# Turning an image batch by 180 degrees: the first store without its hold, all groups in four pieces

## The chip, the cores and the metric

The kernel runs on one core of one Trainium2 chip. The metric is the device time of one execution in microseconds (us). Before the change it is 121.88 us, the median of 3 runs (121.86 to 121.97). The tables and quoted lines below come from one profiled execution of the same kernel.

## What is computed

The input `x` is a float32 array of shape (32, 3, 256, 256), 25.17 MB. Each of the 96 images is turned by 180 degrees:

```python
def reference(x):
    return np.rot90(x, k=2, axes=(-2, -1)).astype(np.float32)
```

An image has 65536 numbers in a row in memory, and turning it by 180 degrees reverses that row from end to end. Nothing is added or multiplied: 25.17 MB are read, put in reverse order and written.

## The kernel before, in words

The 96 images are handled as three groups of 32. A group is held in one SBUF tile of 128 partitions by 16384 numbers (`A`, `Bt`, `Ct`, 64 KB in each partition, 8.39 MB in all): an image is cut into four quarters, and each quarter lies in a partition of its own. A fourth, small tile `T` is the scratch space.

**Loads.** All are issued at the very start (`load`, line 49). Group A comes in two DMAs: the first 512 numbers of every partition through ScalarE's queue (256 KB), the rest (7936 KB) through SyncE's queue. Groups B and C follow with one DMA each on SyncE's queue.

**Turning.** VectorE (DVE) reverses each partition in place. `turn` cuts the half row of 8192 numbers into pieces, and for each piece `swap` makes three copies (`copy`, line 44): the mirrored piece from the right end goes reversed into `T`, the piece from the left goes reversed to the right end, and `T` goes to the left. With four pieces a piece is 2048 numbers and a group takes 12 copies; with six pieces it is 1366 numbers (1362 for the last) and a group takes 18 copies. The copies keep the order in which the program names them: group A, then B, then C.

**Stores.** `store` (line 52) writes a whole group to the output with one DMA on SyncE's queue. Its address pattern runs through the four quarters of each image backwards, so that reversed quarters in reversed order make a reversed image. So every large transfer, the three loads and the three stores, is issued by SyncE and stands in its queue, `q1` in the profile; only the 256 KB piece of group A goes through ScalarE's queue, `q10`.

**What sets the order.** Semaphores that the framework puts in hold each copy until its group is loaded, and each store until its group is turned. One thing is written by hand: `add_manual_dep` makes the store of group A wait for the last copy of group B as well. This is the hold. In the program, the stores of A and B stand ahead of the turning of group C, and SyncE takes its stores in the order A, B, C, so a store that waits also keeps those behind it waiting.

Of the kernel before, what the change touches and what calls it, by code (L numbers as in the profile page):

```python
# [2 lines left out]

os.environ.setdefault("NEURON_RT_ULTRASERVER_MODE", "4")

# [4 lines left out]


@with_exitstack
def kernel(
    ctx: ExitStack,
    tc: tile.TileContext,
    x: bass.AP,
    out: bass.AP,
):
    nc = tc.nc  # L20
    P = 128

    B, C, H, W = x.shape
    L = H * W
    G = 32
    E = L // 4
    J = E // 8

    x4 = x.rearrange("b c h w -> (b c) (h w)").rearrange(
        "(g n) (s e) -> g (n s) e", n=G, s=4)  # L30
    o4 = out.rearrange("b c h w -> (b c) (h w)").rearrange(
        "(g n) (s e) -> g n s e", n=G, s=4)

    pool = ctx.enter_context(tc.tile_pool(name="slots", bufs=1))
    A = pool.tile([P, E], x.dtype, tag="A")
    Bt = pool.tile([P, E], x.dtype, tag="B")
    Ct = pool.tile([P, E], x.dtype, tag="C")
    T = pool.tile([P, J], x.dtype, tag="T")

    def back(t, lo, hi):  # L40
        return t[:, hi - 1:(lo - 1 if lo else None):-1]

    def copy(dst, src):
        c = nc.vector.tensor_copy(out=dst, in_=src)  # L44
        tc.keep_in_program_order(c)
        return c

    def load(t, g, lo=0, hi=E, queue=nc.sync):
        return queue.dma_start(out=t[:, lo:hi], in_=x4[g][:, lo:hi])  # L49

    def store(t, g):
        return nc.sync.dma_start(out=o4[g][:, ::-1, :], in_=t[:, :])

    def swap(t, lo, w):
        hi = E - lo - w
        copy(T[:, 0:w], back(t, hi, hi + w))
        copy(t[:, hi:hi + w], back(t, lo, lo + w))
        return copy(t[:, lo:lo + w], T[:, 0:w])

    half = E // 2  # L60

    load(A, 0, 512, E)
    load(A, 0, 0, 512, nc.scalar)
    load(Bt, 1)
    load(Ct, 2)

    def turn(t, pieces):
        step = -(-half // pieces)
        for lo in range(0, half, step):
            last = swap(t, lo, min(step, half - lo))  # L70
        return last

    turn(A, 4)
    last = turn(Bt, 6)
    tc.add_manual_dep(
        store(A, 0).ins, last.ins.name,
        mybir.DependencyInfo(
            mybir.DependencyClass.Sync, mybir.DependencyReason.DATA),
        reason="the first store goes when the loads are nearly done")
    store(Bt, 1)  # L80
    turn(Ct, 4)
    store(Ct, 2)


# [1 line left out]
_INS = ['x']  # L86
_OUTS = [((32, 3, 256, 256), 'float32')]


# [23 lines left out]
```

## Time and profile before

| what | value |
|---|---|
| median of 3 runs | 121.88 us |
| the three runs | 121.86, 121.88, 121.97 us |
| span of the profiled execution, first to last instruction | 120.1 us (120.07) |
| median less span | 1.8 us |
| VectorE busy | 45.2 us (38%), 42 copies |
| DMA queue q1 | 50.07 MB, 96.9% of the 16 DMA engines' span |
| DMA queue q10 | 0.26 MB, 0.6% |
| moved by DMA in all | 50.33 MB, 419 GB/s over the span |
| copies of group A | 22.69 to 37.79 us, 12 of 1.23 us |
| copies of group B | 42.11 to 58.40 us, 18 of 0.87 us |
| copies of group C | 61.45 to 76.56 us, 12 of 1.23 us |
| stores issued | A 58.43, B 59.10, C 76.59 us |

All times within an execution count from the start of its span. The profiled execution has no separate time of its own in the record beside its span; the medians are of other executions, and the 1.8 us between are what lies ahead of the first and behind the last instruction. A DMA's "us to landing" runs from the start of its issue until its semaphore is full, so it holds the time in which it stands behind other transfers. Besides the views, the trace holds a record of each DMA packet: its queue, size, start and duration. "Packet records" below means these, with the starts counted from the start of the span.

### The profile page before, as it was taken

To read this page: it belongs to the slowest core of one execution; us is meant where nothing else is said; L and a number is where in the kernel's file an instruction comes from. 1 tells how busy PE (TensorE), PEld (TensorE's weight loads), DVE (VectorE), ACT (ScalarE), POOL (GpSimd) and SP (SyncE) were. 2 spreads that over 40 slices of the span, in tenths; PEclk is the share of its full clock that TensorE was granted. 3 is DMA by queue.
4 is the path that set the end of the run, shared out by engine and by line. 5 is a ranking of instruction groups with operands and counts; after the bars stand their busy time and mean duration, and the time that the engine had idled before them with its cause. 6 is when DMAs were issued, how large, how long until landed. Compare 5 with 4: busy or idle time off the path is not lost.

```text
span 120.1 us, 99 instructions
## 1 busy us (share of the span) xinstructions
DVE 45.2 (38%) x42; POOL 0.2 (0%) x4
## 2 busy tenths in 40 slices
DVE  0000000499995099999459999400000000000000
POOL 0000000000000000000000000000000000000000
DMA  9888988899889988998899889988898889888980
GB/s 338 349 349 349 699 349 349 360 633 415 349 349 589 459 349 349 568 480 349 349 502 546 349 349 458 589 349 349 349 699 349 349 349 699 349 349 349 677 371 0
DMA packets 1008, 50.33 MB, mean 419 GB/s; under 512 B 112, under 2 KB 112, under 8 KB 240
## 3 DMA queue, kind: packets, MB, share of 16 engines
q1 hardware_dynamic: 864, 50.07, 96.9%
q10 hardware_dynamic: 144, 0.26, 0.6%
HBM read 25.17 MB, written 25.17 MB: 419 GB/s over the span
## 4 chain that ended last, share of the span: by engine, by line
DMA 34%; DVE 26%; another core or an unknown queue 2%; issue 1%; SPq 0%; DVEq 0%
DMA Bt<-in_x_dram 34%; DVE Bt L44 9%; DVE T L44 9%; DVE Ct L44 8%; SPq L49 0%; DVEq L44 0%
## 5 line engine op out<-in xcount | busy, mean ns | idle before, releaser
L44 DVE COPY T<-A 128x2048 f32<-128x2048 f32 x4 | 4.9, 1227 | 22.8 <-DMA A<-in_x_dram 22.7
L44 DVE COPY T<-Bt 128x1366 f32<-128x1366 f32 (+1 forms) x6 | 5.2, 873 | 4.5 <-DMA Bt<-in_x_dram 4.3
L44 DVE COPY T<-Ct 128x2048 f32<-128x2048 f32 x4 | 4.9, 1227 | 3.2 <-DMA Ct<-in_x_dram 3.1
L44 DVE COPY Bt<-T 128x1366 f32<-128x1366 f32 (+1 forms) x6 | 5.2, 873 | 0.2
L44 DVE COPY Bt<-Bt 128x1366 f32<-128x1366 f32 (+1 forms) x6 | 5.2, 872 | 0.2
L44 DVE COPY Ct<-T 128x2048 f32<-128x2048 f32 x4 | 4.9, 1227 | 0.1
L44 DVE COPY A<-T 128x2048 f32<-128x2048 f32 x4 | 4.9, 1227 | 0.1
L44 DVE COPY Ct<-Ct 128x2048 f32<-128x2048 f32 x4 | 4.9, 1227 | 0.1
L44 DVE COPY A<-A 128x2048 f32<-128x2048 f32 x4 | 4.9, 1226 | 0.1
L97 POOL MEMSET const-bfloat16-1.0<- 128x1 bf16 x1 | 0.1, 102 | 0.0
L97 POOL MEMSET const-uint8-127<- 128x1 uint8 x1 | 0.1, 102 | 0.0
L97 POOL MEMSET const-float32-0.0<- 128x1 f32 x1 | 0.1, 98 | 0.2 <-issue 0.2
L97 POOL MEMSET const-float32-1.0<- 128x1 f32 x1 | 0.1, 98 | 0.0
## 6 DMA issues: line engine op xcount, KB each, us to landing
A<-in_x_dram SPq DMA_DIRECT2D x1, 7936.0 KB, 21.9
A<-in_x_dram ACTq DMA_DIRECT2D x1, 256.0 KB, 22.1
Bt<-in_x_dram SPq DMA_DIRECT2D x1, 40.8
Ct<-in_x_dram SPq DMA_DIRECT2D x1, 59.7
out_dram<-A SPq DMA_DIRECT2D x1, 22.2
out_dram<-Bt SPq DMA_DIRECT2D x1, 40.9
out_dram<-Ct SPq DMA_DIRECT2D x1, 42.7
```

What stands on the lines that cost most here:

```text
L44: c = nc.vector.tensor_copy(out=dst, in_=src)
L97: nc = _bacc.Bacc("TRN2", target_bir_lowering=False, num_devices=1)
```

## The change

The hold is taken away, group B is turned in four pieces as the others are, and the three stores stand behind all copies in the program, in the order A, B, C. Each store then waits for its own group alone. No DMA is added, removed or resized, and each stays on its queue; VectorE makes 36 copies in place of 42.

```diff
     turn(A, 4)
-    last = turn(Bt, 6)
-    tc.add_manual_dep(
-        store(A, 0).ins, last.ins.name,
-        mybir.DependencyInfo(
-            mybir.DependencyClass.Sync, mybir.DependencyReason.DATA),
-        reason="the first store goes when the loads are nearly done")
+    turn(Bt, 4)
+    turn(Ct, 4)
+    store(A, 0)
     store(Bt, 1)
-    turn(Ct, 4)
     store(Ct, 2)
```

## The prediction

> **What bounds the kernel now.** I read the page first: the busy shares, the slices, the DMA queues.
>
> ```profile
> span 120.1 us, 99 instructions
> ...
> DVE  0000000499995099999459999400000000000000
> ...
> DMA  9888988899889988998899889988898889888980
> ...
> q1 hardware_dynamic: 864, 50.07, 96.9%
> ```
>
> The DMA row is full from the first slice to the last but one, while VectorE (DVE) has holes and stops at 76.56 us. So the 16 DMA engines are the bound. Next the DMA issues, with their time to landing, and the timeline around the hold:
>
> ```profile
> Bt<-in_x_dram SPq DMA_DIRECT2D x1, 40.8
> Ct<-in_x_dram SPq DMA_DIRECT2D x1, 59.7
> out_dram<-A SPq DMA_DIRECT2D x1, 22.2
> out_dram<-Bt SPq DMA_DIRECT2D x1, 40.9
> out_dram<-Ct SPq DMA_DIRECT2D x1, 42.7
> ```
>
> ```profile
> 1.18 0.43 SPq L49 DMA_DIRECT2D Bt<-in_x_dram  x1
> 1.65 0.43 SPq L49 DMA_DIRECT2D Ct<-in_x_dram  x1
> ...
> 36.56 1.23 DVE L44 COPY A<-T 128x2048 f32<-128x2048 f32 x1
> ...
> 57.53 0.87 DVE L44 COPY Bt<-T 128x1362 f32<-128x1362 f32 x1
> 58.43 0.63 SPq L52 DMA_DIRECT2D out_dram<-A  x1
> 59.10 0.59 SPq L52 DMA_DIRECT2D out_dram<-Bt  x1
> 61.45 1.23 DVE L44 COPY T<-Ct 128x2048 f32<-128x2048 f32 x1 [3.05 <-DMA Ct<-in_x_dram]
> ...
> 76.59 0.54 SPq L52 DMA_DIRECT2D out_dram<-Ct  x1
> ```
>
> Issue plus time to landing gives the landings: load B 42.0, load C 61.35, store A 80.6, store B 100.0, store C 119.3 us. Each is 19.3 to 19.4 us after the one ahead of it, although B and C were issued half a microsecond apart and store C at 76.59. So the DMAs of SyncE's queue run strictly one after the other, and each takes 19.3 us.
>
> The packet records say why. On each engine a DMA is eight packets of 64 KB and one of 4 bytes that raises the semaphore; a 64 KB packet follows the one before it after 2.414 us, in the loads and in the stores, and 8 x 2.414 = 19.31 us. From one DMA to the next an engine loses 6 to 10 ns. The first packet starts at 1.76 us, the last semaphore packet at 118.93 us, and nothing lies idle between. The chain of waits names the loads and VectorE but leaves out the stores; I take the queue's order instead.
>
> **The change, part by part.**
>
> *The hold goes.* Store A waits then for the copy that starts at 36.56 and lasts 1.23 us, so it is issued at about 37.82 us, 20.6 us earlier. Its first packet can start about 1.03 us after the issue (load A: issued at 0.73, first packet at 1.76), at 38.85 us. But at 38.85 the queue still holds the end of load B and all of load C, whose last semaphore packets start at 60.46 (first engine) to 60.87 us. If the queue keeps its order, store A's packets start where they start now. Now store A is issued at 58.43 and ready at 59.46, 1.0 us ahead of 60.46: the hold leaves no gap that could be closed. Saved: 0.
>
> *Group B in four pieces.* Now 18 copies take 58.40 - 42.11 = 16.29 us. Group A's 12 copies show the new price: 36.56 + 1.23 - 22.69 = 15.10 us. Group B would be turned at 42.11 + 15.10 = 57.21 us, 1.2 us earlier, and store B issued there rather than at 59.10. Its packets are needed when store A's are through, some 19.3 us after 60.46, at 79.8 us. Cover: 21 us. Saved on the path: 0. The copies themselves do not slow the packets: those of load B that ran beside group A's copies took 2.418 us each, the same as those of load B that ran while VectorE waited from 37.79 to 42.11 us.
>
> *The stores stand behind group C's copies in the program.* This matters only to the engine that runs both, and none does: copies are on VectorE, stores on SyncE. Nothing else waits behind the three stores there but the end of the kernel. VectorE starts group C when load C lands, 61.4 us, as now; group C is turned at 76.56 and its store is needed when store B's packets end, 79.8 + 19.3 = 99.1 us. Cover: 99.1 - 77.6 = 21.5 us.
>
> *How much stands in the queue.* At 1.65 us the queue held three loads, 24 large packets for each engine. After the change at most the end of load B, load C and store A stand there, some 18; later load C's end with stores A and B, fewer still. So no depth is reached that the trace has not shown.
>
> *A cost that the trace does not show:* a store waiting for 20 us behind loads. Nearest rows: when store A was issued, the load packets under way (start 58.02 to 58.46 us) took 2.439 to 2.444 us on four engines, not 2.418, and the first store packet took 2.455 us on one. If this is the price of a store that stands in the queue, it would be paid by the nine packets between 38.85 and 60.46: 9 x 0.026 = 0.23 us at the most, or 9 x 0.037 = 0.33 us by the other row. The other end is below nothing: those 22 to 37 ns are no longer paid at the join. I take 0, the row nearest to it being stores B and C, which stand behind other stores for 20 us and whose neighbours still come every 2.414 us.
>
> **Sum:** 0 + 0 + 0 against the span of 120.07 us; with the 1.8 us around it this is the median, 121.88 us. The forecast is no change.
>
> **The rivals.**
>
> *1. The store shares the engines with the loads (slower).* If store A does not queue behind load C but takes turns with it, load C lands late and group C is turned late. For this: packets of different queues do take turns. At the start the small ScalarE packets and the large SyncE packets alternate on every engine, and a ScalarE packet even slips in between the last data packet of load A and its semaphore packet. Against it: load and store have the same queue, q1. And at the join store A, ready at 59.46, would have found load C's last data packet ending at 60.46 and would have gone ahead of load C's semaphore packet; on all 16 engines the semaphore packet came first. Price: load B's data ends 2.4 us later (43.96), and load C then runs at half speed, 2 x 19.31 us, to 82.6 and lands at 83.0. Turned 15.15 us later (98.2), its store is ready at 99.2. The stores A and B keep the engines busy until 99.5, as the work is the same in any order. So with simple turns it costs nothing, with 0.3 us to spare; this is the point from which it decides. If store B is a third party from 60.7 us on, load C's data ends at 91.1, group C is turned at 106.7, its store ready at 107.7: a gap of 8.2 us, so 130.1 us.
>
> *2. A standing store stretches the load packets.* The price is above: up to 0.33 us, 122.2 us. For it are the four stretched packets; against it that the other 12 engines showed 4 ns at the most.
>
> *3. Store A starts reading while the load still writes (faster).* If an engine could read SBUF for the next store while it writes the last of a load, a store known earlier gains. Now store A is ready 1.0 us ahead of the join, so whatever lies within 1.0 us is already had; at most the rest of one packet, 2.4 - 1.0 = 1.4 us, is left: 120.5 us. Against it: an engine's packets at the join follow without overlap (semaphore packet at 60.457, store packet at 60.466 us), as at the joins between loads and between stores, where the successor stood ready for 20 us and more. The Trainium skill has a rule for this side: "DMA: Bandwidth & Descriptors", section "Two DMAs through the same engine are not ordered", says that descriptors of one queue start in order but are pipelined, with separate queues for reading and writing. By it the time could be 120.5 us; the trace agrees with the order of starts, and shows no overlap worth more than some 10 ns at any join, which would leave 121.88.
>
> *4. The change does not do what it says.* The stores now stand behind group C's copies. Should the framework let store A wait for the copies named last rather than for its own group's, it goes at 76.6: the engines idle from 60.9 to 77.6, and the time is 121.88 + 16.7 = 138.6 us. Against it: the first copy of group A starts at 22.69, on its own load, although loads B and C were named before it.
>
> **How the numbers follow.** Forecast, nothing moves: 0.46 (121.65 to 122.1). Rival 1: 0.22, of which 0.04 costs nothing and 0.18 lies evenly between 122.1 and 130.1. Rival 2: 0.14, of which 0.04 stays within the bound. Rival 3: 0.13, of which 0.03 within the bound. Rival 4: 0.05. About 0.2%, 0.24 us, is what a measurement of this kernel can tell from no change. Within it: 0.46 + 0.04 + 0.04 + 0.03 = 0.57; slower: 0.18 + 0.10 + 0.05 = 0.33; faster: 0.10. The range from 120.5 to 124.0 takes in the forecast, rivals 2 and 3, and the cheap part of rival 1 (0.04 and a quarter of 0.18): 0.46 + 0.14 + 0.13 + 0.04 + 0.04 = 0.81. The dear end of rival 1 and rival 4 are left out.
>
> **What would show it.** Right: store A issued at 37.8 with about 42.8 us to landing; store B at 57.2 with some 42.8 us; loads B and C landing at 42.0 and 61.35 as now; packets of 2.414 us throughout. Rival 1: load C lands well after 61.35, and VectorE's hole ahead of group C grows. Rival 2: load packets between 38.85 and 60.46 above 2.418 us. Rival 3: store A lands before 80.6. Rival 4: store A issued at 76.6. I am wrong if any transfer of the queue overtakes another.

## The result and the profile after

The changed kernel takes 122.84 us (median of 3 runs, 122.76 to 122.90) against 121.88 us: 0.96 us slower, a ratio of 1.0075 with a 95% interval from 1.0061 to 1.0088. The profiled execution took 122.76 us with a span of 121.03 us, 0.97 us more than before. The page after, in the lines that answer to those shown of before:

```profile
span 121.0 us, 94 instructions
...
DVE  0000000499994099998039999500000000000000
...
DMA  9888988897779877978989977997799779877980
...
q1 hardware_dynamic: 864, 50.07, 96.8%
```

```profile
Bt<-in_x_dram SPq DMA_DIRECT2D x1, 40.8
Ct<-in_x_dram SPq DMA_DIRECT2D x1, 60.6
out_dram<-A SPq DMA_DIRECT2D x1, 43.8
out_dram<-Bt SPq DMA_DIRECT2D x1, 43.7
out_dram<-Ct SPq DMA_DIRECT2D x1, 42.7
```

Its timeline around the stores:

```profile
37.78 0.63 SPq L52 DMA_DIRECT2D out_dram<-A  x1
...
57.21 0.55 SPq L52 DMA_DIRECT2D out_dram<-Bt  x1
62.34 1.23 DVE L44 COPY T<-Ct 128x2048 f32<-128x2048 f32 x1 [5.15 <-DMA Ct<-in_x_dram]
...
77.46 0.54 SPq L52 DMA_DIRECT2D out_dram<-Ct  x1
```

Stores A and B are issued when the prediction said, 37.78 and 57.21 us, and the queue keeps its order. Load B still needs 40.8 us to landing. But load C needs 60.6 us in place of 59.7, and everything behind it is late by as much: group C starts at 62.34 rather than 61.45 us, and store C is issued at 77.46 rather than 76.59. From load C's landing at 62.25 the stores land at 81.6, 100.9 and 120.2 us, 19.3 us apart as before. So the whole loss arises ahead of load C's landing and behind load B's.

The DMA view of 56 to 66 us shows where. It is cut into 40 slices of 0.25 us, and a packet's bytes are booked where it ends, so each burst is the end of one packet on all 16 engines. Before:

```profile
GB/s 524 0 0 0 0 0 0 0 2359 1835 0 0 0 0 0 0 0 786 2097 1311 0 0 0 0 0 0 0 1835 1573 786 0 0 0 0 0 0 0 2359 1835 0
```

After:

```profile
GB/s 524 0 0 0 0 0 0 0 1573 2621 0 0 0 0 0 0 0 0 0 0 0 1573 1835 786 0 0 0 0 0 0 262 1573 2097 262 0 0 0 0 0 0
```

Both have a burst in slices 9 and 10 (58.0 to 58.5 us), the end of load C's second-last packets. Before, the next burst fills slices 18 to 20, some 2.4 us later; after, slices 22 to 24. That burst is the end of load C's last packets, and only this one is late: the next follows 2.4 us on in both. In the packet records the last packet of load C takes 2.88 to 3.48 us on the 16 engines, 0.87 us more than 2.418 on the mean and 1.06 us at the most; before, it took 0.03 us more at the most. No other packet of load B or load C took more than 0.01 us longer. In what follows, the **stretch** is what a load's last packet takes beyond the usual time of its kind, as the mean over the engines and the most; the usual time is 2.418 us for the 64 KB packets of loads B and C and 2.342 us for the 62 KB packets of load A. A **join** is the place where one DMA of the queue follows another, and the **price** is the time that a join costs.

### The profile page after: what moved, and what is told of

Same layout as the page of the kernel before. It is cut to its first block, busy times and chain, and to the rows that moved or that the text cites. A ratio compares the mean times of both kernels' runs of the same rounds, so it can differ in the third digit from the quotient of the medians.

```text
span 121.0 us, 94 instructions
## 1 busy us (share of the span) xinstructions
DVE 44.2 (37%) x36; POOL 0.2 (0%) x4
## 4 chain that ended last, share of the span: by engine, by line
DMA 34%; DVE 25%; another core or an unknown queue 4%; issue 1%; SPq 0%; DVEq 0%
DMA Bt<-in_x_dram 34%; DVE T L44 8%; DVE Bt L44 8%; DVE Ct L44 8%; SPq L49 0%; DVEq L44 0%
## 5 line engine op out<-in xcount | busy, mean ns | idle before, releaser
L44 DVE COPY T<-Bt 128x2048 f32<-128x2048 f32 x4 | 4.9, 1226 | 4.4 <-DMA Bt<-in_x_dram 4.3
L44 DVE COPY Bt<-T 128x2048 f32<-128x2048 f32 x4 | 4.9, 1227 | 0.1
L44 DVE COPY Bt<-Bt 128x2048 f32<-128x2048 f32 x4 | 4.9, 1227 | 0.1
## 6 DMA issues: line engine op xcount, KB each, us to landing
Bt<-in_x_dram SPq DMA_DIRECT2D x1, 40.8
Ct<-in_x_dram SPq DMA_DIRECT2D x1, 60.6
```

## The experiments

All kernels are told by their difference from the kernel before or the changed kernel; the kernel before, run beside them on the same chips, took 121.80 to 121.94 us (medians). The stretches are those of the one profiled execution of each. The theories are numbered as they come up in the expectations.

**e1: the pieces.** From the changed kernel:

```diff
-    turn(Bt, 4)
+    turn(Bt, 6)
```

> The changed kernel, but group B turned in six pieces as before. Theory 1 (the join): a store that already stands in the queue when the last packet of the load ahead of it starts stretches that packet, once, by about 0.87 us on the mean engine; so 122.8 us, and the last packets of load C at 3.2 to 3.3 us. Theory 2 (standing): the price grows with the time that the store stands behind the load, 0.96 us for about 21 us; so 122.8 us as well. Theory 3 (pieces): the longer copies of group B do it; so 121.9 us.

122.89 us, ratio 1.0084 (1.0069 to 1.0099); stretch 0.96 us, most 1.30. The pieces have nothing to do with it: theory 3 falls. What is left of the change is the hold and the place of the stores in the program; e3 keeps that place, moves the hold alone, and loses as much.

**e2: when the store comes, just late.** From the kernel before:

```diff
-    last = turn(Bt, 6)
+    last = turn(Bt, 4)
```

> The kernel before, with its hold, but group B turned in four pieces: store A is issued at about 57.25 us and ready at about 58.3 us, while the last packets of load C start from 58.02 to 58.46 us on the 16 engines. Theory 1: engines whose last packet starts before the store is ready are not stretched, those that start later are; the slowest engines decide, so between 121.9 and 122.8 us, with two kinds of packets. Theory 2: the store stands 2.2 us, a tenth of the time, so 0.1 us or less: 121.9 to 122.0 us, all packets alike. Theory 3: 122.8 us.

122.52 us, ratio 1.0051 (1.0031 to 1.0072), with the runs spread from 122.13 to 122.91. Store A is issued at 57.39 us; the stretch is 0.30 us, most 0.59, and on the single engines anything between 0.02 and 0.59. So the expectation of two kinds of packets (theory 1) was off, and the tenth of theory 2 as well. Beside e3 (1.07 us) and the kernel before (0.01 us), it says that the price fades out as the store comes later within the last packet's time.

**e3: when the store comes, before the last packet.** From the kernel before, with the last copies of the pieces listed in `done`:

```diff
-    last = turn(Bt, 6)
+    turn(Bt, 6)
+    last = done[-2]
```

> The kernel before, with the hold on the fifth of group B's six pieces in place of the sixth: store A is issued at about 55.7 us and ready at about 56.75 us, after the second-last packets of load C have started (55.6 to 56.05 us) and before the last ones do (58.02 to 58.46 us). Theory 1: the whole price is paid by the last packets, 122.7 to 122.9 us. Theory 2: the store stands 3.7 us of 21, so 0.17 us: 122.05 us. Theory 3: 121.9 us.

122.98 us, ratio 1.0089 (1.0074 to 1.0104); stretch 1.07 us, most 1.41. The store was issued at 55.72 us, 18 us later than in the changed kernel, and costs as much: the price does not grow with the time that the store stands. Theory 2 falls.

**e4: a second join in the same run.** From the changed kernel, load C issued behind store A:

```diff
-    load(Ct, 2)
...
     turn(A, 4)
+    store(A, 0)
+    load(Ct, 2)
     turn(Bt, 4)
     turn(Ct, 4)
-    store(A, 0)
```

> The changed kernel with load C issued behind store A on the same queue, so that the queue runs load A, load B, store A, load C, store B, store C. Store B then stands behind load C from 58 to 80 us, and store A is ready at 38.85 us, while the last packets of load B start from 38.7 to 39.15 us. No engine idles for lack of work, so without a price of the joins it takes 121.9 us. Theory 1: the join of load C and store B costs 0.9 to 1.0 us, the join of load B and store A something between 0 and 1.0 us by engine, and the join of store A and load C, which no trace shows yet, 0 if only a store behind a load costs: 122.8 to 123.9 us. Theory 2: 1.0 us for store B and 0.1 us for store A: 123.0 us, all packets before the join stretched a little or only the last ones by the standing time.

122.86 us, ratio 1.0076 (1.0060 to 1.0093). Load B's last packets, with store A behind them: stretch 0.89 us, most 1.21. Store A to load C: none. But load C's last packets, with store B behind them for 20 us: 0.02 us, most 0.30. Theory 1, that every such join pays, falls; the price was paid once.

**e5, e6, e7: something small first.** Each from the changed kernel, on ScalarE's queue: the first 512 numbers of each partition of group A stored at 26.46 us, behind group A's first piece; a copy from SBUF to SBUF at 1.29 us; a copy from HBM to HBM at 1.18 us, 256 KB each.

```diff
+    nc.scalar.dma_start(out=S2[:, :], in_=S[:, :])              # e6
...
+    nc.scalar.dma_start(out=D[:, :], in_=x4[0][:, 0:512])       # e7
...
-    turn(A, 4)                                                  # e5
+    turn(A, 4, lambda: store(A, 0, 0, 512, nc.scalar))          # e5
...
-    store(A, 0)                                                 # e5
+    store(A, 0, 512, E)                                         # e5
```

> The changed kernel, but the first 512 numbers of each partition of group A go out by a small store of their own (256 KB, ScalarE's queue) as soon as group A's first piece is turned, at about 26.5 us; the large store A has the rest. Theory 1 (the join: every store that stands behind a load costs): load C's last packets are stretched as before, 0.9 us, so 122.8 us. Theory 4 (the first store: the price is paid once in a run, at the first write to HBM, or the first read of SBUF, by each DMA engine, if a load is under way): load C's last packets stay at 2.418 us, and the 0.9 us appear at about 27.5 us on the packets of load B instead (122.8 us), or nowhere, if another queue's wait does not hold up the loads (121.9 us).

> The changed kernel with a small copy of 256 KB from SBUF to SBUF on ScalarE's queue at the start, so that the engines have read SBUF long before store A. It adds 0.6 us of traffic at the rate of the large packets (256 KB of 50.33 MB in 117 us). Theory 1: last packets of load C stretched by 0.9 us, 122.8 + 0.6 = 123.4 us. Theory 4, if the first read of SBUF is what costs: not stretched there, 122.5 us, or 123.4 us with the price paid at the start. Theory 4, if the first write to HBM is what costs: stretched there as before.

> The changed kernel with a small copy of 256 KB from HBM to HBM on ScalarE's queue at the start, so that the engines have written HBM long before store A, to a scratch array and not to the output. 0.6 us of traffic more. Theory 1: last packets of load C stretched by 0.9 us, 123.4 us. Theory 4, if the first write to HBM is what costs: not stretched, 122.5 us, or 123.4 us with the price paid at the start. Theory 4, if the first read of SBUF costs, or the first write to the output array itself: stretched as before, 123.4 us.

122.87, 123.66 and 123.57 us, ratios 1.0079 (1.0064 to 1.0094), 1.0146 (1.0128 to 1.0163) and 1.0137 (1.0122 to 1.0152). In all three load C's last packets are stretched as before: 0.94, 0.88 and 1.09 us. A small transfer on the other queue, of any of the three kinds, does not pay the price in advance, to the output array or elsewhere. Theory 4 falls in this form.

**e8: the store just too late.** From the kernel before:

```diff
-    last = turn(Bt, 6)
+    last = turn(Bt, 8)
```

> The kernel before with group B in eight pieces: 24 copies of about 0.73 us with their gaps, so the hold ends at about 59.6 us and store A is ready at about 60.7 us, as load C's last packets end (60.46 to 60.88 us). All theories: load C's last packets stay at 2.418 us. Theory 1: the engines idle 0.0 to 0.3 us, 121.9 to 122.2 us. Theory 4: if the first store needs about 0.9 us of its own that is hidden in the kernel before, it now shows behind the loads: the first packets of store A start or end some 0.5 to 0.9 us later, 122.4 to 122.8 us.

122.10 us, ratio 1.0015 (1.0006 to 1.0024). Store A is issued at 59.50 us and its first packets start 1.27 us later, 0.24 us on the mean (at most 0.61) behind load C's last ones, which are not stretched. The store's first packets take 2.47 us. So a first store whose packets find the queue empty needs no 0.9 us of its own, and theory 4 has nothing left here.

**e9: nothing behind the store.** From the changed kernel, store B held by the same means until group C's third copy:

> The changed kernel with store B held until the first piece of group C is turned (about 66 us), so that nothing stands in the queue behind store A when load C ends. Still needed at 79.8 us, so the hold itself costs nothing. Theory 5 (depth: a load's last packet is stretched only if the store behind it has something standing behind itself): not stretched, 121.9 us. Theory 6 (first in its queue: the price is paid once for each queue, at its first join from a load to a store) and theory 7 (posting: the price is paid if the store is issued while a load runs, not if it is issued while a store runs): stretched by 0.9 us, 122.85 us.

122.93 us, ratio 1.0095 (1.0070 to 1.0120); stretch 1.13 us, most 1.47. Theory 5 falls.

**e10: a small store on the same queue.** From the changed kernel:

```diff
...
+    nc.gpsimd.memset(S[:, :], 0.0)
+    nc.sync.dma_start(out=D[:, :], in_=S[:, :])
     load(Bt, 1)
```

> The changed kernel with a small store of zeros (256 KB, to a scratch array in HBM) on SyncE's own queue between load A and load B, 0.6 us of traffic more. Theory 6: the price is paid where load A meets the small store, at about 21 us, and load C's last packets stay at 2.418 us; 123.4 us. Theories 5 and 7: load C's last packets are stretched by 0.9 us; and theory 7 has the small store, issued as load A begins, paying as well: 123.4 us, or 124.3 us with both.

123.36 us, ratio 1.0123 (1.0102 to 1.0144). Load A's last packets, with the small store behind them, are stretched by 0.16 us (most 0.33), load C's still by 0.69 us (most 0.92). Theory 6 falls: the first join of the queue pays only a little when what follows is small, and the next one pays most of the price.

**e11: store B issued while load C runs.** From e4, group B in sixteen pieces:

```diff
-    turn(Bt, 4)
+    turn(Bt, 16)
```

> The kernel with load C behind store A in the queue, but group B turned in sixteen pieces, so that store B is issued at about 65 us, while load C runs (61.2 to 80.5 us), and not at 58.4 us, while store A ran. Load B's last packets are stretched as there. Theory 7: load C's last packets are now stretched by 0.9 us too: 123.7 us. Theory 6: they are not, 122.85 us. Theory 5: they are not, since nothing stands behind store B, 122.85 us.

123.43 us, ratio 1.0129 (1.0112 to 1.0146). Store B is issued at 65.02 us. Load B's last packets: 0.67 us (most 1.02); load C's: 0.06 us (most 0.28). Theory 7 falls. The time is 0.6 us more than theory 6 gave. The packet records account for that in the profiled execution (123.29 us): the engine that ends last pays 0.62 us at load B's last packet, 0.54 us at load C's first, which takes 2.96 us on this engine alone, and 0.28 us at load C's last, 1.45 us in all, and its last large packet ends at 120.38 us in place of 118.93. So here the time follows the engine that pays most, not the mean. Why load C's first packet is stretched there is not known.

**e12, e13: how many loads, which store.** From e4, group A loaded again behind load C; from the changed kernel, a full store of zeros behind load A:

```diff
     load(Ct, 2)
+    load(A, 0)                          # e12
...
+    nc.vector.memset(Ct[:, :], 0.0)     # e13
+    store(Ct, 2)                        # e13
     load(Bt, 1)
```

> The kernel with load C behind store A, and behind load C a second load of group A into its tile (for nothing, it is not used), then store B: the queue runs load A, load B, store A, load C, load A again, store B, store C. 19.3 us of traffic more: 121.9 + 19.3 = 141.2 us without a price. The join of load B and store A costs 0.9 us as before. The open join is that of the second load of A and store B, issued at about 62 us, a join behind two loads in a row, with a store run earlier. Theory 8 (lead: on each engine the reads run ahead of the writes; a store behind a load lets the engine read for the store and starves the load's writes, unless a long store earlier has already put the reads far ahead): about 0.05 us there, 142.2 us in all. Theory 9 (length: the price grows with the loads in a row ahead of the join, near 0.1 us behind one, 0.9 us behind two or three): 0.8 to 0.9 us there, 143.0 us.

> The changed kernel with a full store of zeros from tile C (8.39 MB, overwritten later) behind load A, ahead of load B: the queue runs load A, the zeros, load B, load C, store A, store B, store C. 19.3 us of traffic more, so 141.2 us without a price. Joins: load A to the zeros, behind a single load, the first store of the run; and load C to store A, behind two loads, store A standing there for 30 us and more. Theory 8, and theory 10 (the first large store of a run pays, whatever has gone before): 0.9 us at the first join and some 0.05 us at the second, 142.1 us. Theory 9: about 0.1 us at the first and 0.8 to 0.9 us at the second, 142.2 us.

142.29 us in e12: load B's last packets 0.81 us; the second load's, behind two loads in a row and with store B behind them, 0.10 us (most 0.23). 142.99 us in e13: load A's last packets, a single load with the first large store behind it, 0.79 us (most 1.33); load C's, behind two loads, 0.20 us (most 0.51). Theory 9 falls; the first long join pays, the later ones in these two kernels a tenth to a quarter. e13 took 0.9 us more than theory 8 gave: the engine that ends last paid 1.33 and 0.35 us.

**e14, e15: the queue runs dry between.** From the changed kernel: load C goes into tile A once store A has landed. e15 also ties store B behind that load in SyncE's queue by hand.

```diff
-    load(Ct, 2)
...
     turn(A, 4)
+    store(A, 0)
+    reload = load(A, 2)                 # in e14 without the name
     turn(Bt, 4)
-    turn(Ct, 4)
-    store(A, 0)
+    turn(A, 4)
...
-    store(Ct, 2)
+    store(A, 2)
```

> The kernel with two tiles: group C is loaded into tile A once store A has landed, so that the queue runs dry for some 2 us between store A and load C, and store B stands right behind load C. The join of load B and store A costs 0.9 us. At the join of load C and store B: theory 8: the lead is lost when the queue runs dry, so the price is paid again, 0.8 to 0.9 us: 121.9 + 0.9 + 2 + 0.9 = 125.7 us. Theory 10: only the first large store pays, 0.05 us there: 124.8 us. Theory 9: one load in a row, near 0.1 us: 124.9 us.

> The kernel of e14 with the order on SyncE's queue kept by hand, which the framework had changed there: load A, load B, store A, then, once store A has landed, load C into tile A, and store B right behind it. The queue runs dry for some 2 us between store A and load C. Load B's last packets pay 0.8 to 0.9 us. At the join of load C and store B: theory 8 (lead): the lead is lost when the queue runs dry, so 0.7 to 0.9 us again; about 125.5 us. Theory 10 (first large store of the run): 0.2 us or less; about 124.8 us.

In e14 the framework put store B ahead of the load, so there was no second join from a load to a store; it took 139.84 us and says nothing on the question; its one such join, load B to store A, paid 0.79 us (most 1.08). e15 kept the order: 126.59 us. The packets of store A end at 61.84 us on the last engine and load C's begin at 63.16 us on the first, so the queue was dry for 1.3 us; a single engine stood idle for 1.88 us on the mean. Load B's last packets: 0.86 us (most 1.12). Load C's, with store B behind them: 1.22 us, most 1.48. The price is paid a second time, and in full; theory 10 falls. The time is 1.1 us more than theory 8 gave, for a cost that its sum left out: load C's first packets, which found the queue empty, took 0.66 us more than 2.418 (most 1.01). With it, 121.9 + 0.86 + 1.88 + 0.66 + 1.22 = 126.5 us. The DMA view of e15 from 78 to 88 us shows it as it showed the changed kernel's, one burst late among bursts that come every 2.4 us:

```profile
GB/s 262 2359 1311 262 0 0 0 0 0 0 262 2621 1311 0 0 0 0 0 0 0 0 0 0 0 0 1049 2359 786 0 0 0 0 0 0 786 2097 1049 262 0 0
```

From the burst in slices 11 to 13 to that in slices 26 to 28 it is 3.6 us and more. The same view of e4 at its second join, where no gap lay between store A and load C:

```profile
GB/s 1311 1311 1311 0 262 0 0 0 0 0 1835 1573 524 0 0 262 0 0 0 786 1311 1835 0 0 262 0 0 0 0 1311 1311 1311 0 0 262 0 0 0 262 1573
```

The join is the burst in slices 11 to 13; it comes ten slices after the one ahead of it, and the next nine or ten after it: the distance of 2.4 us is kept. Only the single engine that trails (slices 5, 16, 25) falls back by one slice more, the 0.30 us named above.

**e16, e17: reading SBUF or writing HBM.** From the kernel before, a copy of 8.39 MB from HBM to HBM behind load C; and from the changed kernel, without group B, a copy of tile A into tile B, from SBUF to SBUF, behind load C. e17 doesn't load group B: tile B, with group A's numbers, is turned and stored in the place of both groups.

```diff
     load(Ct, 2)
...
+    nc.sync.dma_start(out=D[:, :], in_=x4[0])               # e16
...
+    nc.sync.dma_start(out=Bt[:, :], in_=A[:, :])            # e17
```

> The kernel before, with its hold, and a copy of 8.39 MB from HBM to HBM (a scratch array) behind load C, issued at the start: the queue runs load A, load B, load C, the copy, store A (there for 20 us when its turn comes), store B, store C. 19.3 us of traffic more at the loads' rate, so 141.2 us, and later still if the copy is slower. Theory 8: the copy reads HBM as the loads do and has no faster source, so load C's last packets stay within 0.1 us of 2.418 us; store A behind the copy reads SBUF, so the copy's last packets are stretched by 0.5 to 0.9 us; 142.1 us. Theory 10, if the first large write to HBM pays: load C's last packets are stretched by 0.9 us and the copy's are not; 142.1 us.

> A kernel that leaves out group B: load A, load C, a copy of tile A into tile B from SBUF to SBUF issued as load A lands (about 22.8 us), so that it stands behind load C for 16 us and more; then tile B is turned and stored in the place of groups A and B, and C as before. Nothing writes to HBM at the join of load C and the copy. Theory 8 (what stands behind reads SBUF): load C's last packets, from about 38.6 us, are stretched by 0.6 to 1.0 us. If the writing to HBM were needed as well, they stay at 2.418 us. The time itself (some 137 us, with a gap while tile B is turned) says nothing.

In e16 the copy stands behind load C from 2 us on, and load C's last packets are stretched by 0.02 us (most 0.03). Its DMA view of 56 to 66 us has them end in slices 18 to 20, 2.4 us after the burst ahead, as in the kernel before:

```profile
GB/s 524 0 0 0 0 0 0 786 1049 2097 262 0 0 0 0 0 0 786 2359 1049 0 0 0 0 0 0 0 1311 2359 524 0 0 0 0 0 0 0 262 786 1573
```

(The copy itself is slow, 2.4 to 4.2 us for a packet, so the join behind it can't be read, and the time of 146.68 us says nothing.) In e17, whose one run of 148.85 us says nothing of the price either, load C's last packets, with the SBUF copy behind them, are stretched by 1.11 us, most 1.64, though nothing writes to HBM there. The DMA issues of e17, whose load C is the second DMA of its queue like load B in the kernel before, show it on the page:

```profile
Ct<-in_x_dram SPq DMA_DIRECT2D x1, 42.2
Bt<-A SPq DMA_DIRECT2D x1, 48.2
```

42.2 us to landing where load B before needed 40.8. So in these two runs the price goes with what the DMA behind the load reads, SBUF and not HBM; writing to HBM is neither needed (e17) nor enough (e16).

**What is settled, and what is not.** The runs show when the price is due: a large DMA that reads SBUF stands behind a load well before the load's last packet ends; the load's last packets are then stretched by 0.7 to 1.2 us, once, and hardly again until the queue has run dry. They fit theory 8. By it, the reading side of each engine goes on to the next DMA while the load's last bytes are still to come, the SBUF reads take its capacity, and the writing side has nothing to write for a while; after that the reads are ahead and stay ahead. For this speaks that in the changed kernel all 368 packets behind the first store packet take 2.418 us or less, none more, while before 74 of them take a little more, and in e8, where the store's packets found the queue empty, 333. But the packet records do not tell reads from writes, so the lead itself is argued and not shown, and neither is why its size is 0.9 us. Open stays the spread from 0.7 to 1.2 us between kernels with the same join. Each stretch is that of a single execution, and the times of one and the same kernel lie as far apart (e4 122.71 to 123.35 us, e9 122.85 to 123.54 us), so it may be a spread between executions.

No version beat the kernel before: the release of store A at 57.39, 58.43 and 59.50 us (e2, before, e8) gave 122.52, 121.9 and 122.10 us, so of these three the hold of the kernel before is the one without a price.

## Why the prediction was wrong

*The bound and the order* were right: the DMA engines are the bound, SyncE's queue keeps its order, and no transfer overtook another.

*"The hold goes ... If the queue keeps its order, store A's packets start where they start now ... Saved: 0"* is the step that failed. The condition held and the conclusion did not: store A's packets start 0.9 us later, because load C's last packets end later. I took the joins between loads and between stores, which cost about 10 ns with the successor standing for 20 us, as a price for every join. The trace had no join from a load to a store that stood there in time; the one that it had was made by the hold.

*The cost that the trace does not show* was looked for in the right place and mis-sized; this is the term of the sum that was put at 0 and is 0.96 us. The upper end, 0.33 us, came from nine packets at 26 or 37 ns each; measured is one packet at 874 ns on the mean engine and 10 ns at the most on any of the others. The "nearest rows" of 22 to 37 ns told nothing of a standing store: the store arrived when these packets were more than half through, and in the same trace the last packets of store A, with store B behind them, are stretched as much (five of them, up to 2.442 us). e2 and e3 show load C's last packets growing by 0.30 and 1.07 us as the store arrives 1.0 and 2.7 us earlier. I then took the end at 0, by the stores B and C, which stand behind stores: the wrong neighbour, since e16 and e17 show that the kind of transfer behind the load decides, and e4 and e15 that what ran ahead of it does too.

*Group B in four pieces* and *the order in the program* cost nothing, as predicted: the loss is the same with six pieces (e1: 122.89 us) and with the order of before (e3: 122.98 us). Store B was issued at 57.21 us, as worked out. *The depth of the queue* was no matter either (e9).

*The rivals.* Rival 2, a standing store that stretches the load packets, was the right kind, with a chance of 0.14 and a price a third of the measured one. Rival 1 and rival 4 did not happen. Rival 3 named what theory 8 takes for the cause and turned its sign: if theory 8 holds, the store is begun early, and that is what costs. The Trainium skill, "DMA: Bandwidth & Descriptors", section "Two DMAs through the same engine are not ordered", has the engine's reading and writing sides as separate queues. The runs agree as far as e16 and e17 go, in which only what the next DMA reads matters (0.02 against 1.11 us); that this slows the load ahead is in the runs and not in that section.

The range, 120.5 to 124.0, held the time by luck, through the room left for the cheap part of rival 1, which did not happen; the forecast of no change did not hold, since the interval begins at 1.0061.

## What to carry to other kernels

On a queue that never runs dry, "issued early" is not free just because the transfer must wait its turn: here a store that stood behind a load cost 0.9 us once, and the hold that released it some two microseconds before the load's end saved that. Price a join by a join of the same kind, load to store or store to store, and where the trace has none, say that the row is missing and keep the range open by a good part of a packet's time. A hold of this kind has a window: 1.0 us too early cost 0.6 us, 1.1 us too late cost 0.2 us.

## What the runs showed of the hardware that I had not expected

- Behind a load, a large DMA that reads SBUF stretches the load's last 64 KB packet from 2.418 us by 0.7 to 1.2 us (0.67 in e11, 1.22 in e15); one that reads HBM by 0.02 us (e16).
- A load whose packets find the queue empty has its first ones stretched by 0.66 us (e15); a store by 0.05 us (e8).
- The price comes back when the queue has been dry for only 1.3 us (e15: 0.86 us, then 1.22 us); without a break it fell to 0.02 to 0.20 us (e4, e11, e12, e13).
- A copy of 8.39 MB from HBM to HBM ran at 2.4 to 4.2 us for each 64 KB packet, where loads and stores need 2.418 us.
- A store of 8.39 MB whose packets found the queue empty had the first of them under way 1.27 us after the issue began (e8), not the 1.03 us that I took from a load. The difference is the issue itself, 0.63 us against 0.39: from its end to the first packet it is 0.64 us in both. So in the kernel before, store A was ready at about 59.7 us and not at 59.46.
